# Weight splits issued by a thread of their own, a third buffer for token copies, and later emission times in a planned kernel

## The chip, the cores and the metric

The kernel runs on one core of a Trainium2 chip. The metric is the device time of one launch in microseconds. A core has five engines with a queue each: TensorE (PE, its weight loads PEld), VectorE (DVE), ScalarE (ACT), GpSimd (POOL) and SyncE (SP), which here issues nearly all DMAs. An engine works through its queue in the order in which the program emitted the instructions; where one waits, those behind it wait too.

## What is computed

One inference step of a hybrid encoder layer on 512 prompt frames and 32 sample frames (544 columns), with model width 1024:

```
u    = RMSNorm(h)
proj = u @ w_in                      # 102 column blocks of 128
SSD:  conv -> silu -> state-space recurrence (16 heads x 64, state 128) -> gated RMSNorm with silu(z)
GLA:  4 heads, per-channel forget gate, recurrence -> head RMSNorm times silu(gate)
RWKV: 16 heads x 64, delta rule S_t = S diag(w) - (S kk)(kk a)^T + v k^T -> LayerNorm, bonus, silu(gate)
m    = sum_i sigmoid(merge_i) * (o_i @ P_i)
h    = h + m @ w_out
h    = h + CrossAttention(RMSNorm(h), memory)      # 256 memory tokens
y    = RMSNorm_final(h)
```

The memory's keys and values are computed first. All states are outputs too.

## The kernel before

**The planner.** `body` emits the whole program from cooperating Python generators, called threads here. `Sched` keeps a modelled time for each engine and for the DMAs, and every emitted instruction moves its engine's time on. `Sched.run` resumes the first thread in order of priority (lowest number first) whose wait is over by the modelled time of PE. A thread gives up its turn by `yield`: with a number it sleeps for so many modelled nanoseconds, with a function it sleeps until that is true. `S.at(a)` is the modelled time until tile `a` is written, for a DMA its modelled landing. None of this exists on the chip: the threads decide only in which order instructions stand in the engines' queues. What an instruction truly waits for are semaphores on its operands and on its output buffer's earlier readers.

**Dense blocks.** The 166 weight blocks of 1024x128 (512 KB each) pass through `dense`, the thread of lowest priority (9). Float32 products are made of three float32r products: a high part `wh` and a low part `wl = w - wh` of the weights, and the same two parts of the activations. A block over 544 columns is two halves of 24 matmuls. `load_w` issues the DMA into one of three `wraw` buffers, `split_w` makes the parts: ACT copies `wraw` to `wh`, and a small thread `low` of priority -1 then has DVE subtract. `commit` keeps a list `ahead` of loaded blocks; it takes from three queues in order (jobs of the stage, convolution blocks, and `fill`: 56 gate blocks that depend on `u` alone, of which the last 8 are held back for the end of the second stage). `take` removes from `ahead` the first block whose input is ready and splits it. In `dense`, `more(1)` takes the next block at two places: at the top of the loop, after a block is finished, and right after a block is begun. After each 5 matmuls (`GRAIN`) the thread gives up its turn, and so other threads' small matmuls come in between.

**Stages.** 0 to 65 us: memory keys and values, RMSNorm. 65 to about 660: RWKV in eight pairs of heads, by five threads. `rw_A` prepares a pair (key norms, decays, scan, products of a pair's tokens), and its helper `tokens` transposes three operands on PE (`ptk`), copies them by ACT into a buffer `tm`, and stores them by four DMAs each into the slot tile `NK`; a last copy `t8` (named `t` in the profile) takes the tail tokens through the same ring of buffers, `TMB = 2` of them. Only then does `rw_A` begin the next pair (`w2h`, then `sq`, `k` and the norm matmuls `pn`). `rw_I` inverts triangular 32x32 blocks on POOL (31 steps of `im` and `td`), `rw_J` loads the inverse as `TT`, has DVE transpose it (`x`, L1122) and finishes the 64x64 inverse on PE, `rw_C` runs the recurrence over 9 chunks, `rw_N` normalises. From about 660 to 925: GLA and SSD, beside the convolution blocks, the query and key blocks of GLA and what is left of `fill`. From 925: `gates` (priority 1) loads each branch's result `yt` and gate `gt` (272 KB each, `gt` in 3 buffers, two tiles ahead), multiplies them on DVE and splits the product into parts `o__`; first RWKV (`gated`), then GLA (`gated`), then SSD (`ssd_norm`, which also sums squares, and splits only after the last RWKV projection). The output projections `prwkv`, `pgla`, `pssd` need all eight tiles of their branch; each half block is gated by DVE with a loaded `mgt` into `macc`. Then `wout`, `wq`, attention and `wo` follow, whose weights are kept in parts `wr`.

`S.at` and the ring of a tile tag are what the change turns on:

```
def at(self, *aps):
    return max(0.0, max(self.since(a, 0) for a in aps) - self.t["pe"])
...
if c % W["GRAIN"] == 0 and c < 24:
    commit()
    yield None
```

Of the kernel before, what the change touches and what calls it, by code (L numbers as in the profile page):

```python
# [11 lines left out]
AF = mybir.ActivationFunctionType  # L12
# [34 lines left out]
       ("a", "v"): 145.0, ("a", "p"): 170.0, ("v", "a"): 130.0, ("v", "p"): 155.0, ("p", "v"): 70.0, ("p", "a"): 65.0,  # L47
       ("a", "q"): 150.0, ("v", "q"): 150.0, ("p", "q"): 150.0, ("v", "v"): 127.0, ("a", "a"): 153.0, ("p", "p"): 102.0}

W = dict(HOLD1=0, HOLD2=8, CALM=3000, EARLY1=1, DEPTH1=3, EARLY2=2, FAIR=1500, GRAIN=5, IS=900.0, IE=0, NQ=3000, XL=2, SG=6, PRW=800.0, R2=0.0, DE=2500.0, T2=0, FA=900.0, XM=3000.0, WARM=12, KM=1500.0)  # L50


class Cols:
# [286 lines left out]
def body(tc, I, O):  # L340
    nc = tc.nc
    S = Sched(nc)
# [17 lines left out]
    with tc.manual_schedule(), \  # L360
# [107 lines left out]
        ahead = []  # L468
# [20 lines left out]
        def split_w(j):  # L489
            blk = j["blk"]  # L490
            if blk in spl or blk in splitting:
                return
            tag, w = raw.pop(blk)
            if "res" in j:
                h, l = (pools["res"][1].tile([128, 1088], F32R, name="wr", tag=t) for t in j["res"])
            else:
                k = wn[0] % 2
                wn[0] += 1
                h, l = (base.tile([128, 1088], F32R, name=n_, tag=f"{n_}{k}") for n_ in ("wh", "wl"))
            h, l = h[:, :1024], l[:, :1024]  # L500
            S.act(h, w, AF.Copy)
            hl = tuple(a.rearrange("p (a b) -> p a b", b=128) for a in (h, l))

            def low():
                yield S.at(h)
                S.tt(l, w, f32(h), SUB)
                free_raw[tag] = S.since(w, 1)
                done.add(f"split {blk}")
                spl[blk] = hl

            splitting.add(blk)
            S.add(low(), -1)

        def commit():
            while len(ahead) < look["depth"]:
                q = next((q for q in queues if q and ready(q[0])), None)
                if q is None:
                    if sum(not ready(j) for j in ahead) >= look["early"]:
                        return
                    q = next((q for q in queues if q), None)  # L520
                if q is None or not load_w(q[0]["blk"]):
                    return
                ahead.append(q.pop(0))
# [20 lines left out]
        def dense():  # L544

            nxt = []

            def more(n):
                j = take() if len(nxt) < n else None
                if j is not None:  # L550
                    nxt.append(j)

            while True:
                commit()
                more(1)
                if not nxt:
                    presplit()
                    if not ahead and "end" in done:
                        return
                    yield lambda: any(ready(j) for j in ahead) or (commit() or any(ready(j) for j in ahead)) or "end" in done  # L560
                    continue
                cur = nxt.pop(0)
                commit()
                more(1)
                presplit()
                yield lambda: cur["blk"] in spl
                h, l = spl[cur["blk"]]
                if "res" not in cur:
                    del spl[cur["blk"]]
                    splitting.discard(cur["blk"])  # L570
                x = cur["x"]
                m = cur.get("m", 128)
                hv = cur.get("hv", ((0,) + HV[0], (1,) + HV[1]))
                if "late" in cur:
                    yield lambda: n_late[0] < 3
                    n_late[0] += 1
                for hi, o, w in hv:
                    ps = pd.tile([128, 512], F32, name="pd", tag="pd")
                    yield max(S.at(h), S.since(ps, 1) - S.t["pe"])
                    c = 0  # L580
                    for kb, part in [(kb, part) for kb in range(8) for part in (0, 1)] + [(kb, 2) for kb in range(8)]:
                        if c == 16:
                            yield S.at(l)
                        a = l if part == 2 else h
                        S.mm(ps[:m, :w], a[:, kb, :m], x(kb, o, w)[part % 2], start=c == 0, stop=c == 23)
                        c += 1
                        if c % W["GRAIN"] == 0 and c < 24:
                            commit()
                            yield None
                    if hi == hv[-1][0] and W["T2"]:  # L590
                        commit()
                        more(2)
                    if "late" in cur:
                        S.add(late(cur, ps), -0.5)
                        continue
                    if "ucond" in cur:
                        yield cur["ucond"]
                    cur["use"](hi, ps)
                    done.add(f"{cur['blk']}:{hi}")
                    yield None  # L600
                done.add(cur["blk"])
# [288 lines left out]
            return a.rearrange("p (c t) -> p c t", t=64)  # L890

        HP = ((0, 288), (288, 288))
        TMB = 2

        def rw_A(p):

# [214 lines left out]
        def rw_J(p):  # L1111

            yield has(f"rwJ{p}")
            rwr = pools["rwR"][1]
            d = slot[p % NSLOT]
            nk, tt_ = d["NK"], d["TT"]
            for h in range(2):
                S.dma(out=tt_[h * 64:h * 64 + 64, :, h * 64:h * 64 + 64], in_=rows64(d_scr, h))
            yield S.at(tt_)
            x1 = rwr.tile([128, 8, 32], F32, name="x1", tag="xw")  # L1120
            for h in (0, 64):
                nc.vector.transpose(x1[h:h + 64], tt_[h:h + 64, 0:8, h:h + 32])  # L1122
                S.note("v", 340, (x1[h:h + 64],), (tt_[h:h + 64],))
            yield S.at(x1) + W["XM"]
            ps = yield from bank("pW")
            for c in range(8):
                for h in (0, 64):
                    S.mm(ps[h:h + 64, c * 32:c * 32 + 32], nk[h:h + 32, c, h // 64, h // 32, :], x1[h:h + 32, c, :], True, True)
            w = rwr.tile([128, 8, 32], F32, name="W", tag="xw")
            S.act(w.rearrange("p c j -> p (c j)"), ps[:, :256], AF.Copy)  # L1130
            yield S.at(w)
            ps = yield from bank("pT")
            for c in range(8):
                for h in (0, 64):
                    S.mm(ps[h:h + 32, c * 32:c * 32 + 32], w[h + 32:h + 64, c, :], tt_[h + 32:h + 64, c, h + 32:h + 64], True, True)
            for h in (0, 64):
                S.act(tt_[h:h + 32, 0:8, h + 32:h + 64], ps[h:h + 32, :256].rearrange("p (c t) -> p c t", t=32), AF.Copy)
            done.add(f"rwI{p}")
            yield None
# [536 lines left out]
        def gated(br, t):  # L1676

            yield has(*[f"{dict(rwkv='rg', gla='gg')[br]}{j}" for j in range(8)])
            low = None
            for j, (yt, gt) in enumerate(gate_loads(br)):  # L1680
                yield S.at(yt, gt)
                S.stt(yt, yt, 0.5, gt, MUL, MUL)
                if low:
                    low()
                low = split_o(br, t, j, yt)
                yield S.free("v")
            low()
            done.add(f"O{br}")

        def ssd_norm(t):  # L1690

            gp = pools["gate"][1]
            yield has(*[f"z{j}" for j in range(8)])
            ys, rr = [], []
            for j, (yt, gt) in enumerate(gate_loads("ssd")):
                yield S.at(yt, gt)
                S.stt(yt, yt, 0.5, gt, MUL, MUL)
                if j % 4 == 0:
                    sq = gp.tile([128, T], F32, name="nsq", tag="nsq")
                S.act(gt if j % 4 else sq, yt, AF.Square)  # L1700
                if j % 4:
                    S.tt(sq, sq, gt, ADD)
                ys.append(yt)
                yield S.free("v")
                if j % 4 == 3:
                    yield S.at(sq)
                    r = gp.tile([128, T], F32, name="nrr", tag="nrr", bufs=2)
                    rr.append(r)
                    rstd(r, sq, HV, 512)
            yield has("prwkv7")  # L1710
            low = None
            for j, y in enumerate(ys):
                S.stt(y, y, Pm("g_ssd", j), rr[j // 4], MUL, MUL)
                if low:
                    low()
                low = split_o("ssd", t, j, y)
                yield S.free("v")
            low()
# [404 lines left out]
```

## Time and profile before

| | |
|---|---|
| time, median of 3 runs | 1303.99 us (1301.09 to 1306.32) |
| the profiled execution's own time | 1301.87 us |
| its span, first to last instruction | 1300.1 us |
| PE busy, matmuls | 1260.5 us, 97% |
| PE busy, weight loads | 1215.3 us, 93% |
| DVE, ACT, POOL busy | 65%, 48%, 28% |
| mean granted TensorE clock | 0.99 |
| moved by DMA | 181.11 MB, 45.1% of 16 engines' time |

Times in the rows are microseconds from the span's start. A row of a timeline gives start, duration, engine, line, operation, output<-inputs and shapes, and in brackets how long the engine had been idle and what ended that. A row of the waits gives who waited for whom: total us, times, longest us. Line L245 is the one line from which all plain matmuls are emitted, L278 all ACT work, L284 and L293 most DVE work, L327 all DMAs; the tile names tell them apart.

### The profile page before, as it was taken

How to read it: one execution, taken by the hardware profiler on the slowest of the kernel's cores; microseconds unless marked ns; L12 is line 12 of the kernel's file. 1: busy time of each engine (PE TensorE's matmuls, PEld its weight loads, DVE VectorE, ACT ScalarE, POOL GpSimd, SP SyncE). 2: the span in 40 equal slices, each digit the busy share in tenths (PEclk: the TensorE clock that was granted, in tenths of full speed). 3: DMA queues.
4: the chain of work that ended last, by engine and by line, in shares of the span. 5: the costliest groups of instructions: out<-in, count | busy, mean ns of one | idle time of the engine just before them, and what ended most of it. 6: DMA issues, size and time to landing. Idle time of an engine off the chain costs nothing.

```text
span 1300.1 us, 27497 instructions
## 1 busy us (share of the span) xinstructions
PE 1260.5 (97%) x10848; PEld 1215.3 (93%) x10848; DVE 838.8 (65%) x1666; ACT 627.3 (48%) x1191; POOL 361.6 (28%) x706
## 2 busy tenths in 40 slices
PE   8999989999999999999999999989999999999997
PEld 8999989999998999999999999978999999999997
DVE  6857747675858586844456586877665846575543
ACT  6664534557373637444364646364444423544422
POOL 0012837375656645551001062432100000000000
PEclk8999989999999999999999999999999999999999
DMA  8644462727363635364253243343887445540302
GB/s 291 190 129 111 131 147 64 182 75 183 84 167 96 156 96 151 99 174 134 101 191 114 76 127 109 103 135 114 277 311 251 141 144 181 171 146 25 106 17 70
DMA packets 170385, 181.11 MB, mean 139 GB/s; under 512 B 100480, under 2 KB 123104, under 8 KB 170128
## 3 DMA queue, kind: packets, MB, share of 16 engines
q1 hardware_dynamic: 169824, 178.68, 45.1%
q8 instruction: 86, 1.41, 0.5%
q10 hardware_dynamic: 432, 0.67, 0.2%
q14 instruction: 43, 0.35, 0.1%
HBM read 136.27 MB, written 35.39 MB: 132 GB/s over the span
## 4 chain that ended last, share of the span: by engine, by line
PE 54%; DVE 7%; ACT 2%; issue 1%; POOL 1%; DMA 0%; POOLq 0%; DVEq 0%; ACTq 0%; SPq 0%
PE pd L245 42%; PE pc L245 2%; PE psc L245 1%; PE pov L245 1%; PE py L245 1%; PE pO L245 1%; DVE wl L284 1%; DVE acc L293 1%; PE ph L245 1%; DVE AR L284 1%; PE pT L242 1%; PE pss L245 1%; PE pS L245 0%; DVE seg L299 0%; PE pp L245 0%
## 5 line engine op out<-in xcount | busy, mean ns | idle before, releaser
L245 PE MATMUL pd<-ul,wh 128*128 128x272 f32 (+1 forms) x1632 | 434.5, 295 | 0.0
L245 PE MATMUL pd<-uh,wh 128*128 128x272 f32 (+1 forms) x1632 | 431.1, 294 | 3.1 <-ACT wh L278 2.3
L245 PEld LDWEIGHTS pd<-uh,wh 128*128 128x128 f32 (+1 forms) x1632 | 307.1, 188 | 6.9 <-ACT wh L278 2.8
L245 PEld LDWEIGHTS pd<-ul,wh 128*128 128x128 f32 (+1 forms) x1632 | 307.4, 188 | 3.0 <-issue 1.5
L245 PE MATMUL pd<-uh,wl 128*128 128x272 f32 (+1 forms) x1632 | 251.4, 291 | 0.0
L245 PEld LDWEIGHTS pd<-uh,wl 128*128 128x128 f32 (+1 forms) x1632 | 219.9, 188 | 2.7 <-issue 1.4
L284 DVE TENSOR_TENSOR wl<-wraw,wh 128x1024 fp32r<-128x1024 f32 (+1 forms) x143 | 182.2, 1277 | 29.7 <-ACT wh L278 28.2
L278 ACT ACTIVATE wh<-wraw 128x1024 fp32r<-128x1024 f32 (+1 forms) x143 | 149.3, 1047 | 44.9 <-PE pd L245 27.4
L284 POOL TENSOR_TENSOR im<-td,nd 108x84 f32<-108x84 f32 (+23 forms) x248 | 110.8, 447 | 176.4 <-DMA td<-in_eye 86.5
L245 PE MATMUL pd<-uh,wr 128*128 128x256 f32 (+1 forms) x768 | 148.6, 291 | 1.4 <-ACT uh L278 1.4
L245 PEld LDWEIGHTS pd<-uh,wr 128*128 128x128 f32 x768 | 121.0, 188 | 3.0 <-ACT uh L278 1.6
L284 POOL TENSOR_TENSOR td<-td,im 108x84 f32<-108x84 f32 (+23 forms) x248 | 117.5, 474 | 19.4
L284 POOL TENSOR_TENSOR macc<-macc,hrs 128x288 f32<-128x288 f32 x3 | 2.3, 792 | 372.6 <-DVE macc L293 372.6
L245 PE MATMUL pd<-ul,wr 128*128 128x256 f32 (+1 forms) x384 | 100.2, 292 | 0.1
L245 PEld LDWEIGHTS pd<-ul,wr 128*128 128x128 f32 x384 | 72.4, 188 | 1.0 <-issue 0.4
L278 ACT ACTIVATE lerpA<-pd,par 128x272 f32<-128x272 f32 x50 | 24.4, 487 | 71.1 <-PE pd L245 60.2
L278 ACT ACTIVATE fg<-pd 128x272 f32<-128x272 f32 x64 | 25.3, 397 | 66.2 <-PE pd L245 56.0
L293 DVE SCALAR_TENSOR_TENSOR Sb<-Sb,GC,pc 64x64 f32<-64x64 f32 x128 | 35.7, 279 | 32.3 <-PE pc L245 30.3
L278 ACT ACTIVATE NK<-pc 128x128 f32<-128x128 f32 x136 | 30.5, 275 | 46.3 <-DVE Sb L293 44.5
L278 ACT ACT_TABLE_LOAD x39 | 50.0, 1283 | 3.9 <-DVE tB L284 1.6
L293 DVE SCALAR_TENSOR_TENSOR fg<-fg,pd 128x272 f32<-128x272 f32 x48 | 20.7, 433 | 47.5 <-ACT fg L278 47.2
L278 ACT ACTIVATE fg<-pd,dpar 128x272 f32<-128x272 f32 x48 | 23.3, 486 | 51.0 <-PE pd L245 46.6
(469 smaller groups left out, 2461.1 us busy)
## 6 DMA issues: line engine op xcount, KB each, us to landing
wraw<-in_wall SPq DMA_DIRECT2D x165, 512.0 KB
g_mg<-fg SPq DMA_DIRECT2D x24, 272.0 KB
mgt<-g_mg SPq DMA_DIRECT2D x24, 272.0 KB
NK<-tm SPq DMA_DIRECT2D x96, 64.0 KB
ab<-acs_d SPq DMA_DIRECT2D x8, 512.0 KB
nd<-n_scr SPq DMA_DIRECT2D x24, 144.0 KB
n_scr<-NK SPq DMA_DIRECT2D x16, 144.0 KB
TT<-d_scr SPq DMA_DIRECT2D x16, 144.0 KB
```

Of the source, the lines that this page charges most:

```text
L242: self.nc.tensor.transpose(out, lhsT, rhs)
L245: self.nc.tensor.matmul(out, lhsT, rhs, start=start, stop=stop, skip_group_check=shared)
L278: self.nc.scalar.activation(out=out, in_=in_, func=f, scale=scale, bias=bias)
L284: eng.tensor_tensor(out=out, in0=a, in1=b, op=op)
L293: self.nc.vector.scalar_tensor_tensor(out=out, in0=a, scalar=s, in1=b, op0=op0, op1=op1)
```

## The change

Five edits. The thread `low` now waits until the raw weights have landed by the plan and only then emits ACT's copy to the high part; before, `split_w` emitted the copy at once. Inside a block, after each 5 matmuls, `dense` takes the next block if it has none, if the first block in `ahead` is ready, and if that block's load has landed by the plan. The ring for token copies has 3 buffers instead of 2. The thread `rw_J` sleeps 1500 ns more after the planned landing of `TT`. The gating of GLA and of SSD sleeps 2000 ns more for each of its 16 tiles after the planned landing of `yt` and `gt`.

```
-W = dict(..., KM=1500.0)
+W = dict(..., KM=1500.0, TM=1500.0, GM=2000.0)
...
 def split_w(j):
...
-            S.act(h, w, AF.Copy)
             hl = tuple(a.rearrange("p (a b) -> p a b", b=128) for a in (h, l))
 
             def low():
+                yield S.at(w)
+                S.act(h, w, AF.Copy)
                 yield S.at(h)
                 S.tt(l, w, f32(h), SUB)
...
                         if c % W["GRAIN"] == 0 and c < 24:
                             commit()
+                            if not nxt and any(ready(j) and (j["blk"] in spl or j["blk"] in splitting or S.at(raw[j["blk"]][1]) == 0.0) for j in ahead[:1]):
+                                more(1)
                             yield None
...
-        TMB = 2
+        TMB = 3
...
-            yield S.at(tt_)
+            yield S.at(tt_) + W["TM"]
             x1 = rwr.tile([128, 8, 32], F32, name="x1", tag="xw")
...
-                yield S.at(yt, gt)
+                yield S.at(yt, gt) + (W["GM"] if br == "gla" else 0.0)
...
-                yield S.at(yt, gt)
+                yield S.at(yt, gt) + W["GM"]
```

## Rows read from the trace of the kernel before

**Rows 1.** The page: busy time of each engine, and the granted clock in 40 slices of the span (tenths of full speed).

```profile
PE 1260.5 (97%) x10848; PEld 1215.3 (93%) x10848; DVE 838.8 (65%) x1666; ACT 627.3 (48%) x1191; POOL 361.6 (28%) x706
PEclk8999989999999999999999999999999999999999
```

**Rows 2.** Windows by stage: length, busy us (and count) of PE, PEld, DVE, ACT and POOL, granted clock, DMA share, GB/s.

```profile
65.00:100.00 35.00, 35.00 (x282) 35.00 (x281) 20.73 (x39) 21.89 (x37) 6.58 (x11) 1.00 0.40 120
100.00:660.00 560.00, 543.54 (x5155) 524.67 (x5155) 363.09 (x753) 277.32 (x562) 273.80 (x572) 0.99 0.47 127
660.00:925.00 265.00, 258.74 (x2180) 241.97 (x2179) 186.81 (x367) 141.20 (x251) 77.22 (x102) 0.99 0.39 125
925.00:960.00 35.00, 32.81 (x255) 32.62 (x254) 22.62 (x29) 17.12 (x28) 0.00 (x0) 0.97 0.99 348
```

**Rows 3.** Waits of PE over the whole span, the first four of the list.

```profile
PE pc L245 <- DVE R L284: 4.4, 7, 1.2
PE pn L245 <- ACT k L278: 4.1, 1, 4.1
PE pd L245 <- DVE kv L284: 2.5, 1, 2.5
...
PE pd L245 <- ACT wh L278: 2.3, 3, 1.5
```

**Rows 4.** Timelines around 184 us: ACT's copies of the second pair, the DMAs of its token copies on SP, and PE.

```profile
167.37 1.09 ACT L278 ACTIVATE tm<-ptk 128x512 f32<-128x512 f32 x2 [1.85 <-PE ptk L242]
...
181.55 5.28 SPq L327 DMA_DIRECT2D NK<-tm  x8
...
185.83 0.48 ACT L278 ACTIVATE t<-ptk 64x384 f32<-64x384 f32 x1 [5.64 <-DMA NK<-tm]
...
187.32 0.68 ACT L278 ACTIVATE k<-sq 128x576 fp32r<-128x576 f32 x1
...
188.05 0.61 PE L245 MATMUL pn<-k,blk 128*128 128x288 f32 x1 [4.10 <-ACT k L278]
```

**Rows 5.** Two windows of PE alone in which the granted clock is at its lower level: length, busy us (count), clock, DMA share, GB/s.

```profile
186.40:193.10 6.70, 4.86 (x20) 0.50 0.87 219
...
957.80:961.10 3.30, 3.30 (x17) 0.50 0.99 333
```

**Rows 6.** ACT's timeline: the last token copy `tm` and the tail copy `t` of a further pair.

```profile
366.21 0.60 ACT L278 ACTIVATE tm<-ptk 128x512 f32<-128x512 f32 x1 [0.29 <-PE ptk L242]
...
376.75 0.47 ACT L278 ACTIVATE t<-ptk 64x384 f32<-64x384 f32 x1
```

**Rows 7.** Two places where PE ran out of dense work: DVE's rows that made the next block ready, ACT's copies of its weights, PE's first matmul.

```profile
906.13 1.12 DVE L293 SCALAR_TENSOR_TENSOR ys<-xs,par,py 128x128 f32<-128x128 f32 x4 [0.16 <-PE py L245]
...
914.77 0.40 PE L245 MATMUL pd<-uh,wh 128*128 128x272 f32 x1 [1.52 <-ACT wh L278]
...
949.85 0.72 DVE L284 TENSOR_TENSOR o__12118<-yt,o__12118 128x544 fp32r<-128x544 f32 x1
...
955.12 2.00 ACT L278 ACTIVATE wh<-wraw 128x1024 fp32r<-128x1024 f32 x2
...
956.27 0.49 PE L245 MATMUL pd<-o__11911,wh 128*128 128x272 f32 x2 [2.19 <-issue]
```

**Rows 8.** What follows there: SP's issue of the first merge gates, and DVE's first use of them.

```profile
958.98 0.90 SPq L327 DMA_DIRECT2D mgt<-g_mg  x2
...
965.09 0.78 DVE L293 SCALAR_TENSOR_TENSOR macc<-mgt,pd 128x272 f32<-128x272 f32 x2 [5.26 <-DMA mgt<-g_mg]
```

**Rows 9.** The gating of GLA and SSD: its 16 products (duration in ns, first and last start), DVE's last low part of SSD, and PE's first matmul of the SSD projection.

```profile
L293 DVE SCALAR_TENSOR_TENSOR yt<-yt,gt x16: 716/719/726, 951.8 to 1009.1; 128x544 f32<-128x544 f32 x16
...
1034.39 0.72 DVE L284 TENSOR_TENSOR o__13071<-yt,o__13071 128x544 fp32r<-128x544 f32 x1
...
1055.91 0.41 PE L245 MATMUL pd<-o__12857,wh 128*128 128x272 f32 x2
```

**Rows 10.** Timelines of ACT and DVE near 20 us.

```profile
19.14 1.06 ACT L278 ACTIVATE wh<-wraw 128x1024 fp32r<-128x1024 f32 x1 [2.98 <-DMA wraw<-in_wall]
...
21.04 1.09 DVE L284 TENSOR_TENSOR kv<-pd,rsm 128x256 f32<-128x256 f32 x3 [2.42 <-ACT rsm L278]
```

**Rows 11.** Waits of ACT and DVE for the loads that the change is about.

```profile
ACT wh L278 <- DMA wraw<-in_wall: 10.6, 5, 3.0
...
DVE x L1122 <- DMA TT<-d_scr: 7.8, 7, 2.2
...
ACT wr L278 <- DMA wraw<-in_wall: 6.3, 6, 2.3
...
DVE yt L293 <- DMA gt<-g_gla: 2.1, 2, 1.3
```

**Rows 12.** PE's timeline in the second stage, where it had no dense block.

```profile
846.85 0.63 PE L242 MATMUL pT<-con,g_gl 128*128 128x128 f32 x4 [1.30 <-DVE g_gl L284]
...
859.16 0.49 PE L245 MATMUL pO<-g_qe,gS 128*128 128x128 f32 x2 [1.23 <-DVE gS L305]
```

**Rows 13.** Two of the 25 us windows of the RWKV stage, that with the fullest DVE and that with the most PE idle time but for the one of rows 4 (columns as in rows 2), and POOL's steps of the inverse (ns: least, median, most).

```profile
200.00:225.00 25.00, 24.77 (x195) 24.01 (x195) 22.96 (x47) 9.48 (x21) 20.88 (x33) 1.00 0.23 77
...
400.00:425.00 25.00, 23.14 (x196) 21.83 (x197) 19.78 (x48) 6.91 (x17) 10.23 (x21) 1.00 0.42 115
...
L284 POOL TENSOR_TENSOR td<-td,im x248: 222/348/2068, 126.3 to 590.5; 108x84 f32<-108x84 f32 x12, 108x54 f32<-108x54 f32 x8, 108x90 f32<-108x90 f32 x8, 108x72 f32<-108x72 f32 x8
```

More of the change, by code (lines that the diff above doesn't have):

```diff
@@ L48 @@
        ("a", "q"): 150.0, ("v", "q"): 150.0, ("p", "q"): 150.0, ("v", "v"): 127.0, ("a", "a"): 153.0, ("p", "p"): 102.0}
-W = dict(HOLD1=0, HOLD2=8, CALM=3000, EARLY1=1, DEPTH1=3, EARLY2=2, FAIR=1500, GRAIN=5, IS=900.0, IE=0, NQ=3000, XL=2, SG=6, PRW=800.0, R2=0.0, DE=2500.0, T2=0, FA=900.0, XM=3000.0, WARM=12, KM=1500.0)
+W = dict(HOLD1=0, HOLD2=8, CALM=3000, EARLY1=1, DEPTH1=3, EARLY2=2, FAIR=1500, GRAIN=5, IS=900.0, IE=0, NQ=3000, XL=2, SG=6, PRW=800.0, R2=0.0, DE=2500.0, T2=0, FA=900.0, XM=3000.0, WARM=12, KM=1500.0, TM=1500.0, GM=2000.0)
 class Cols:
@@ L500, in split_w @@
             h, l = h[:, :1024], l[:, :1024]
-            S.act(h, w, AF.Copy)
             hl = tuple(a.rearrange("p (a b) -> p a b", b=128) for a in (h, l))
             def low():
+                yield S.at(w)
+                S.act(h, w, AF.Copy)
                 yield S.at(h)
@@ L588, in dense @@
                             commit()
+                            if not nxt and any(ready(j) and (j["blk"] in spl or j["blk"] in splitting or S.at(raw[j["blk"]][1]) == 0.0) for j in ahead[:1]):
+                                more(1)
                             yield None
@@ L892, in body @@
         HP = ((0, 288), (288, 288))
-        TMB = 2
+        TMB = 3
         def rw_A(p):
@@ L1118, in rw_J @@
                 S.dma(out=tt_[h * 64:h * 64 + 64, :, h * 64:h * 64 + 64], in_=rows64(d_scr, h))
-            yield S.at(tt_)
+            yield S.at(tt_) + W["TM"]
             x1 = rwr.tile([128, 8, 32], F32, name="x1", tag="xw")
@@ L1680, in gated @@
             for j, (yt, gt) in enumerate(gate_loads(br)):
-                yield S.at(yt, gt)
+                yield S.at(yt, gt) + (W["GM"] if br == "gla" else 0.0)
                 S.stt(yt, yt, 0.5, gt, MUL, MUL)
@@ L1695, in ssd_norm @@
             for j, (yt, gt) in enumerate(gate_loads("ssd")):
-                yield S.at(yt, gt)
+                yield S.at(yt, gt) + W["GM"]
                 S.stt(yt, yt, 0.5, gt, MUL, MUL)
```

## The prediction, made blind

> **What bounds the kernel now.** I read the page first, then PE's waits, then windows by stage, then the timelines around each of PE's stops. On the page PE is busy for 97% of the span and no other engine for more than 65%, and the clock line is at 9 but for the first and the sixth slice [rows 1]. So the kernel is bound by PE's work, and what can be won is PE's idle time: 1300.1 - 1260.5 = 39.6 us, and what the lower clock costs after some of the stops. The windows say where: 16.5 us idle in the RWKV stage, 6.3 in the GLA and SSD stage, 2.2 in the 35 us of the gating [rows 2]; the rest is at the start and at the very end. The list of PE's waits [rows 3] shows that few are long: a norm matmul waits 4.1 us for ACT's `k`, a dense block 2.5 us for DVE's `kv`, and dense blocks 2.3 us for `wh`. No engine is overloaded at these places; each is an instruction that stood in the wrong place of a queue.
>
> **Third buffer for token copies.** The stop at 184 us reads backwards like this [rows 4]. PE's `pn` waits for ACT's `k`. ACT reached `k` late because the tail copy `t` before it in ACT's queue stood for 5.64 us, until the DMAs `NK<-tm` were done. With two buffers `t` overwrites the one from which the copy before the last is being stored, and SP issued those eight stores only from 181.55 on. With three, `t` takes the buffer of the pair's first copy, whose own copy stands two before. So the wait of 5.64 us goes, `k` moves ahead by more than the 4.10 us that PE idled, and the 4.10 us go whole. What is late next is DVE's second part of `k`, 0.2 us; I count nothing for it. Just after the stop the granted clock stood at 0.50, that is 1.2 instead of 2.4 GHz, and PE worked 4.86 us there [rows 5]; at the upper level that work takes half, so 2.4 us come back. Sum: -6.5 us.
>
> The same ring also holds up the thread `rw_A`: in this pair `t` ends 18 us after the last `tm` began, and in another it starts 10.5 us after it without a wait that the profile shows [rows 4, 6]; there the plan itself waits for the stores, and the next pair begins only after `t`. All pairs will begin earlier. As PE is full of dense work in this stage this gives no time by itself: it uses fewer fill blocks early and leaves them for the second stage. I take the stage as some 30 us shorter (a slot is free only when the recurrence of three pairs before is done, so not all of 8 x 10 us), which is five blocks.
>
> What those blocks are worth: in the second stage PE idled 1.30 and 1.23 us at places where it had no dense block [rows 12]. Between 0 and -2.5 us; I take half, -1.2. What they cost: the same DVE work in 530 instead of 560 us. The stage now idles 16.5 us, 12.4 of it outside the stop [rows 2, 4]. I take +1.5, bounds 0 and, as a rival below, the worst window.
>
> **Taking the next block inside a block.** Twice PE ran out because the next block's input became ready while the current block was running, and its weights were split only after that block [rows 7]. The products that free the held fill blocks were ready at 907 us, but PE started the block at 914.77 after 1.52 us idle. RWKV's last gated part was ready at 950.6; ACT split the first projection's weights at 955.12, and PE idled 2.19 us. With the new test the split comes at the next group of 5 matmuls, and both stops go: 1.52 + 2.19 = 3.7 us, and half of the 3.30 us at the lower clock after the second [rows 5], 1.65. Sum: -5.4 us. The split moves ACT's and DVE's work (about 1 and 1.2 us) ahead of the current block's evacuation, and the next 512 KB load with it. Where PE is always busy a matmul takes 35.00 / 282 = 0.124 us [rows 2], a half block of 24 thus 3.0 us, and three PSUM buffers hide a delay of 1 us. What is late next is the merge gate: issued at 958.98, landed by 965.09 [rows 8]. PE may run three halves, 9 us, before DVE must have used it, until about 963 if PE starts at 954.1. If the issue moves ahead by the same 2.2 us it is in time; if it stays, up to 2.2 us of the gain are given back. I take it as in time, since it is issued when the first half is evacuated.
>
> **High part by the thread.** ACT waits 10.6 us in 5 places and 6.3 us in 6 places for raw weights [rows 11] and holds back what stands behind. Only one of these shows in PE: at 19.14 ACT stood 2.98 us, the norm factor `rsm` behind it was late, DVE's `kv` after it, and PE waited 2.5 us for the bank [rows 3, 10]. But the block that PE wanted then needed those same weights, whose split ended at 20.20; so not the whole wait can go. Bounds 0 and 2.5 us; I take -0.5. On the other side a split emitted after the planned landing can fall behind another ACT operation, and the raw buffer's next load, queued on SP behind the subtraction, comes later too. Behind one `k` of 0.68 us each [rows 4] the 11 places would cost 7.5 us if each were just in time; between taking a block and using it lies a block of 48 matmuls, 6 us, so I take 0.
>
> **Later transposes and later gating.** DVE stood 7.8 us in 7 places for `TT` and 2.1 us in 2 for GLA's gates [rows 11], with other work behind it; PE idled at none of these. TM adds 1.5 us to each of 8 inverses; PE has fill blocks to do meanwhile, so 0; without that cover 12 us at most. GM adds 2 us to each of 16 tiles in one thread. Their products run from 951.8 to 1009.1, that is 3.8 us each; SSD's parts are done at 1035.1, and PE needs them at 1055.91, so 20.8 us are free [rows 9], 17.0 after PE loses 3.8 us just before. Bounds: nothing, if the waits only replace waits for the landing, and 16 x 2 = 32 us, if they add in full. `gt` has three buffers, so three loads are under way, and 2 us added to a chain over three tiles make 0.67 each, 10.7 in all. That is hidden; I take 0.
>
> **The sum.** -6.5 - 1.2 + 1.5 - 5.4 - 0.5 = -12.1 us. Against the profiled execution's own 1301.9 us this gives 1289.8; its time was 2.1 us under the median of the three runs, so I predict 1292 us.
>
> **The rivals.** First, *the gating of SSD comes too late*. If GM adds in full, the parts are ready 32 - 17.0 = 15.0 us after PE wants them, at a point with no other dense work: 1292 + 15 = 1307. It decides from 17.0 / 16 = 1.1 us added per tile. For it speaks that one thread handles all tiles in turn; against it the pace of 3.8 us, longer than the 2 us added. Chance 0.12.
>
> Second, *the first stage gets too dense*, which ends slower. DVE is busy 363 of 560 us there, and PE's most frequent wait is for DVE's `R` [rows 2, 3]. If every 25 us idle like the worst ordinary window, 1.86 us [rows 13], that is 22.4 x 1.86 = 41.7 us instead of 12.4, +29.3: 1292 - 1.5 + 29.3 = 1320. It makes the kernel slower by over 0.5% when the mean reaches 1.45 us (12.4 + 1.5 + 18.5 = 32.4 us over 22.4 windows). Against it: the window with the fullest DVE, 22.96 of 25 us, idles 0.23 [rows 13]. POOL's steps speak for it: `td` takes 222 ns at least and 2068 at most [rows 13], so something holds POOL at times. The Trainium skill (SBUF — State Buffer, "SBUF: two separate sides") says that a DVE instruction with two SBUF inputs and a GpSimd instruction that reads SBUF take a shared port pair as an exclusive lock, so that one of them blocks; the spread agrees with it, and by that rule closer packing would lengthen the inverse, and the recurrence that waits for it, as in this rival. Chance 0.13.
>
> Third, *the stop only moves*: with the orders all shifted, another norm or projection meets an equal wait, or the second place of rows 7 isn't reached in time. Then only one group of the gains is left, 5.4 or 6.5 us: 1304 - 6 = 1298, within 0.5%. Chance 0.16.
>
> How much room there is, is itself in doubt: by PE's matmuls 39.6 us are idle, by its weight loads 1300.1 - 1215.3 = 84.8. The Trainium skill (Perfetto Trace Analysis, its opening note) says that matmul busy time is the bad measure and the weight loads' share the good one; by that rule more than my sum could be won.
>
> **How the numbers follow.** The forecast has 0.59, the rivals 0.12, 0.13 and 0.16. A difference under 0.5%, 6.5 us, can hardly be told from none here. The forecast alone lies between 1283 (all bounds in its favour: 2.0 more at the start, 1.3 in the second stage, 1.5 for no crowding, and 4, a sixth of the 26.8 us for which ACT and DVE stand in rows 11, should some of these count for PE after all) and 1297. With the first and third rival the range is 1283 to 1307; above it lies most of the second rival, below it little. Faster by over 0.5%: the forecast, and a little of the third rival, 0.60; within 0.5%: most of the third and the first, 0.25; slower: the second, and a late gating with further loss, 0.15.
>
> **What would show it.** Right: `t` no longer waits for `NK<-tm`, and the last `t` comes well before 571 us; the 4.1 us wait of `pn` and the lower clock after it are gone; PE starts the first projection without a gap of 2 us; ACT's waits for `wraw` and DVE's for `TT` shrink; PE's idle time falls from 39.6 to about 29 us. Wrong: a gap of PE before the SSD projection; more idle time from 100 to 640 us in waits for `R` or `Sb`; a new stop of several us with the lower clock behind it; PE's `pd` waiting for `wh` more often than 3 times.

## The result and the profile after

The changed kernel took 1293.3 us (median; 1292.3 to 1293.5) and the kernel before 1304.6 beside it (1301.1 to 1306.3): a ratio of 0.9928, 95% interval 0.9905 to 0.9951 (the two medians alone give 0.991, inside it). Predicted were 1292 us. The profiled execution took 1293.31 us with a span of 1291.5, against 1301.87 and 1300.1 before.

The page after, PE's busy time and the granted clock in 40 slices [rows 1]:

```profile
PE 1256.5 (97%) x10848; PEld 1214.8 (94%) x10848; DVE 837.9 (65%) x1666; ACT 623.5 (48%) x1189; POOL 363.4 (28%) x706
PEclk9999989999999999999999999999999999999999
```

PE's idle time is 1291.5 - 1256.5 = 35.0 us, where it was 39.6. The prediction had about 29. The windows by stage, with PE alone (length, busy us and count, clock, DMA share, GB/s), say where it fell [rows 2]:

```profile
100.00:660.00 560.00, 541.42 (x5152) 0.99 0.47 130
660.00:925.00 265.00, 262.36 (x2198) 0.99 0.40 123
925.00:960.00 35.00, 35.00 (x282) 1.00 0.92 326
```

The first window idles 18.6 us, where it was 16.5: nothing was won in the RWKV stage, in which I had placed half of the gain. The second went from 6.3 to 2.6 and the third from 2.2 to 0. The other 4.0 us are busy time; what made the same 10848 matmuls shorter I did not find.

PE's longest waits after [rows 3]:

```profile
PE pT L245 <- ACT W L278: 4.3, 1, 4.3
PE pd L245 <- ACT wh L278: 4.1, 4, 1.3
PE pc L245 <- DVE R L284: 3.9, 4, 1.7
PE pc L245 <- DVE Sb L293: 3.7, 1, 3.7
```

Here `W` belongs to the inverse, and `R` and `Sb` to the recurrence. `pn <- k` and `pd <- kv` are off the head of the list, as predicted, but a stop of the same size stands 7 us earlier. This is its neighbourhood in the timelines of SP, ACT and PE (start, duration, then the idle time before the instruction and what ended it):

```profile
162.56 1.31 SPq L327 DMA_DIRECT2D d_scr<-td  x3
...
166.99 2.85 SPq L327 DMA_DIRECT2D nd<-n_scr  x3
...
171.25 2.62 SPq L327 DMA_DIRECT2D NK<-tm  x4
173.97 0.55 SPq L327 DMA_DIRECT2D wraw<-in_wall  x1
...
177.67 1.06 ACT L278 ACTIVATE wh<-wraw 128x1024 fp32r<-128x1024 f32 x1 [7.25 <-DMA wraw<-in_wall]
...
180.30 0.37 ACT L278 ACTIVATE W<-pW 128x256 f32<-128x256 f32 x1
...
180.72 1.06 PE L245 MATMUL pT<-TT,W 32*32 32x32 f32 x32 [4.25 <-ACT W L278]
```

Read backwards: PE's `pT` waits for ACT's `W`; ACT is late because the split `wh` before it stood 7.25 us for its raw weights; and SP issued that load only at 173.97, after a run of DMAs that begins at 162.56 with the stores of the inverse's result `td`. In the kernel before, the token copy `t` stood there for its buffer [rows 4]; now a weight split stands there for its load. The clock fell to its lower level again, too, as it did before [rows 5]:

```profile
178.70:185.50 6.80, 4.78 (x68) 0.50 0.60 169
```

ACT's waits for raw weights at `wh` rose from 10.6 us in 5 places [rows 11] to this:

```profile
ACT wh L278 <- DMA wraw<-in_wall: 31.5, 12, 7.2
```

Those at `wr` are off the list; with one at `hs`, of 2.2 us, the sum is 33.7 us, where it was 16.9.

Two more rows matter below (count, duration in ns, first and last start). The first, by the tile `t`, is ACT's copy in all eight pairs; the last began at 571.6 before:

```profile
L278 ACT ACTIVATE t<-ptk x8: 472/481/486, 115.2 to 537.8; 64x384 f32<-64x384 f32 x8
```

The second, by the tile `g_ssd`, gives SP's stores of the eight `z` blocks, the last fill blocks that may run early; the last started at 823.8 before, and it was the only one after 705 us:

```profile
L327 SPq DMA_DIRECT2D g_ssd<-fg x8: 319/323/382, 657.0 to 862.4; - x8
```

### The profile page after: what moved, and what is told of

The parts are those of the page before. It is cut to its first block, busy times and chain, and to the rows that moved or that the text cites. A ratio compares the mean times of both kernels' runs of the same rounds, so it can differ in the third digit from the quotient of the medians.

```text
span 1291.5 us, 27500 instructions
## 1 busy us (share of the span) xinstructions
PE 1256.5 (97%) x10848; PEld 1214.8 (94%) x10848; DVE 837.9 (65%) x1666; ACT 623.5 (48%) x1189; POOL 363.4 (28%) x706
## 4 chain that ended last, share of the span: by engine, by line
PE 60%; DVE 4%; ACT 1%; issue 1%; POOL 0%; POOLq 0%; ACTq 0%; DVEq 0%
PE pd L245 46%; PE pc L245 3%; PE psc L245 1%; PE pO L245 1%; PE py L245 1%; PE pov L245 1%; PE ph L245 1%; DVE wl L284 1%; PE pS L245 1%; PE pss L245 1%; PE pT L242 1%; DVE acc L293 0%; PE pl L245 0%; PE pp L245 0%; DVE AR L284 0%
## 5 line engine op out<-in xcount | busy, mean ns | idle before, releaser
L284 DVE TENSOR_TENSOR wl<-wraw,wh 128x1024 fp32r<-128x1024 f32 (+1 forms) x143 | 176.8, 1238 | 43.4 <-ACT wh L278 42.8
L284 POOL TENSOR_TENSOR td<-td,im 108x84 f32<-108x84 f32 (+23 forms) x248 | 114.3, 461 | 19.4
L278 ACT ACTIVATE NK<-pc 128x128 f32<-128x128 f32 x136 | 30.4, 274 | 30.8 <-DVE Sb L293 27.3
```

The costliest lines, as they stand in the source:

```text
L278: self.nc.scalar.activation(out=out, in_=in_, func=f, scale=scale, bias=bias)
L284: eng.tensor_tensor(out=out, in0=a, in1=b, op=op)
```

## Each part alone, on the kernel before

```diff
 a1_ring3     TMB = 2 -> 3
 a2_midtake   + if not nxt and any(ready(j) and ... for j in ahead[:1]): more(1)
 a3_thread    S.act(h, w, AF.Copy) moved into low(), behind yield S.at(w)
 a4_times     TM = 1500, GM = 2000
```

**The third buffer alone.** Expected:

> The kernel before with the third buffer for token copies alone. By the sum: the tail copy never waits for the stores, the stop of 4.1 us near 184 us and the lower clock behind it (2.4 us) are gone, and the second stage idles a little less: 6 us faster, about 1298.5 us, PE idle 33 to 35 us. By the rival that the stop only moves, as the trace of the changed kernel suggests (SP's queue is late with the stores, and the next weight load stands behind them): another stop of 3 to 6 us with the lower clock behind it between 150 and 400 us, in which ACT stands for raw weights; the gain is then 0 to 3 us, 1302 to 1305 us.

Measured: 1314.5 us, ratio 1.0102 [1.0073, 1.0131]. It is slower by 13 us. The largest stop is at the same place again, behind a third ACT instruction:

```profile
190.22 0.40 ACT L278 ACTIVATE fg<-pd 128x272 f32<-128x272 f32 x1 [13.14 <-DMA g_rwkv<-fg]
...
191.15 0.60 PE L245 MATMUL pd<-uh,wh 128*128 128x272 f32 x1 [7.38 <-DVE fg L293]
```

Here, in ACT's and PE's timelines, a gate copy `fg` waits 13.14 us for the store of the tile that it overwrites. That store, too, is one of SP's. Neither expectation has this time. A second stop, of 5.47 us at 419, stands where DVE waits 3.71 us for `TT`, the wait that TM is meant for.

**The mid-block take alone.** Expected:

> The kernel before with the taking of the next block inside a block alone. By the sum: PE's gaps of 1.52 us (before the first held fill block) and 2.19 us (before the first RWKV projection) go, and with the second the lower clock behind it, 1.65 us: 5.4 us faster, 1299 us; the first 800 us of the trace as before. By the rival that the merge gate is late next: the second gap comes back as a wait of PE for a PSUM bank some 9 us later, 3 us faster only, 1301.5 us.

Measured: 1293.6 us, ratio 0.9958 [0.9936, 0.9980], which is 5.5 us. The gaps at 913 and 954 us are gone [rows 7], and no wait for the merge gate came in their place: PE idles 0.4 us from 925 to 960.

**The thread alone.** Expected:

> The kernel before with the high part emitted by the thread alone. By the sum: PE's wait for kv at 19 us shrinks from 2.5 to about 0.5 us, nothing else: 1304 us, between 1302 and 1305. ACT's waits for raw weights, 16.9 us in all, should shrink if the planned landing is right. By the rival that the plan's landings are too early when SP is behind: ACT's waits for raw weights do not shrink, or grow as in the changed kernel, where ACT stood 31.5 us for wh; the time is then within 3 us of the kernel before, either way.

Measured: 1298.7 us, ratio 0.9991 [0.9967, 1.0014]. PE's stop at 19 us fell from 2.55 to 0.47 us; ACT's waits for raw weights hardly shrank (16.9 to 16.0 us in all), and the time is that of the kernel before within the interval, as the rival has it.

**The added times alone.** Expected:

> The kernel before with the two later times alone (1500 ns at the inverse's transpose, 2000 ns at the gating of GLA and SSD). By the sum: 0, 1303 to 1306 us; DVE's wait of 7.8 us for TT goes, the SSD parts are ready about 11 us later against PE's first SSD projection, so that 9 to 10 of the 20.8 us are left. By the rival of the late gating: 32 us later, PE stands some 11 us before the SSD projection, 1316 us.

Measured: 1315.9 us, ratio 1.0115 [1.0083, 1.0146]: slower by 15 us. The RWKV stage ended 10 us later, all `z` blocks were used by 698 us, and PE stopped 7.4 us near 916 us where no dense block was left. The time is the rival's 1316, but not its cause: before the SSD projection, where the late gating would show, PE has no gap over 0.3 us.

By the ratios the four add up to 13 - 5.5 - 1 + 15 = +21 us (the -1 is not clear of noise), and together they give -9. So the parts act on one another, and the next runs take one away at a time.

## One part taken away from the changed kernel

**The ring back to two buffers (TMB = 2).** Expected:

> The changed kernel with two buffers for token copies again (TMB = 2), all else as changed. Theory A, the parts add: alone the third buffer cost 13 us, so without it the kernel takes 1293 - 13 = 1280 us. Theory B, the ring pays only beside TM (alone it brought DVE stops at TT and a stage that was only 4 us shorter, while with TM the stage was 16 us shorter and blocks were left for the second stage): without it the RWKV stage ends later than in the changed kernel (its last gate product after 652 us instead of 636), no block is left after 800 us, PE idles over 6 us from 660 to 925, and the time is 1300 us or more. Prediction's own term: 6.5 us at the stop, so 1299 to 1300.

Measured: 1315.5 us, ratio 1.0115 [1.0088, 1.0143]. Theory A, that the parts add, falls by 35 us; theory B holds in all its signs. The last step of the recurrence ended at 666 us, where it was 637 with the ring. The stores of the `z` blocks:

```profile
L327 SPq DMA_DIRECT2D g_ssd<-fg x8: 319/320/381, 653.1 to 701.8; - x8
```

PE's window of the second stage:

```profile
660.00:925.00 265.00, 252.69 (x2088) 0.98 0.37 119
```

PE's largest stop, from its timeline:

```profile
926.16 1.98 PE L245 MATMUL py<-seg,xc 128*64 128x128 f32 x16 [6.32 <-DVE seg L284]
```

The ring's use beside the other parts is to be seen here. Without it the stage is 29 us longer, PE fills these 29 us with `z` blocks, and none is left after 702; in the second stage PE then idles 12.3 us, where the changed kernel with its four blocks after 830 idles 2.6. Over the whole span PE idles 8.3 us more than in the changed kernel and is busy for 12.6 us more; of the latter the lower clock makes some 8, estimated as half of the difference between 34.1 and 17.9 us of work at the lower level. The wait for `seg` (DVE itself waits there for the load of `ab`) has no like in the changed kernel, where PE's idle time of this stage is 2.6 us in all.

**Without the mid-block take.** Expected:

> The changed kernel without the taking of the next block inside a block. Theory A, the part's worth is local (the gaps before the second stage's dense blocks and before the first projection): the gaps near 910 and 950 us are back, 1.5 and 2.2 us with lower clock after the second, and the time is 1293 + 5.4 = 1299 us, as in the run of this part alone, which gave 5.5. Theory B, with z blocks left over in the second stage the first of these gaps has cover: only the gating's gap comes back, 1293 + 3.8 = 1297. If the time is that of the changed kernel within 1 us, the part owed its gain to the new order that it made.

Measured: 1296.7 us, ratio 0.9966 [0.9951, 0.9982], 0.0038 x 1301 = 4.9 us over the changed kernel's ratio; the two intervals just touch. One gap came back, not two, and larger:

```profile
910.65 0.59 PE L245 MATMUL pd<-uh,wh 128*128 128x272 f32 x1 [4.20 <-ACT wh L278]
```

The size fits both theories. The place is A's first gap; its second, before the first projection, did not come back, and B had it the other way round.

**Without the thread.** Expected:

> The changed kernel with the high part emitted as before, at once, and not by the thread. Theory A: the thread's copy is worth the kv stop at 19 us alone, 2.1 us, so 1295 us, with ACT's waits for raw weights as long as in the changed kernel (some 30 us in 12 places), since these come from loads that stand behind token stores on SP. Theory B: the thread holds other orders up; without it the waits for raw weights fall to 15 us or less and the time to 1290.

Measured: 1299.5 us, ratio 0.9990 [0.9968, 1.0011]; its ten times spread from 1292.6 to 1305.4, and the profiled one is the lowest. So the size is uncertain, some 8 us by the ratios. The waits for raw weights fell to 17.2 us in 10 places, nearly as B has it, but the time rose, as A has it, and more than A has it. The stop at 19 us is back with 2.78 us. The stop near 180 us is there again, three times as long and again behind `fg`:

```profile
188.55 0.40 ACT L278 ACTIVATE fg<-pd 128x272 f32<-128x272 f32 x1 [16.13 <-DMA g_rwkv<-fg]
...
190.85 1.07 PE L245 MATMUL pT<-TT,W 32*32 32x32 f32 x32 [11.98 <-ACT W L278]
```

**Without GM.** Expected:

> The changed kernel with GM = 0, no added time at the gates of GLA and SSD. Theory A (GM is hidden but for the last microsecond): the two halves of the gating end some 10 to 17 us earlier, about 1010 instead of 1026, the 0.9 us gap of PE at 1048 goes, and the time is 1292. Theory B (GM keeps gate products away from ACT and DVE work that PE needs in the second stage): DVE's waits for gates return and PE idles more from 660 to 960, so 1297 or more.

Measured: 1290.8 us, ratio 0.9914 [0.9893, 0.9936]. This is theory A, though by the intervals it can't be told from the changed kernel. The last high part of SSD's gating starts at 1020.26 without GM. With it, in the changed kernel, the same part and PE's first matmul of the SSD projection are:

```profile
1047.54 0.66 ACT L278 ACTIVATE o__13297<-yt 128x544 fp32r<-128x544 f32 x1 [1.50 <-DVE yt L293]
...
1049.20 0.52 PE L245 MATMUL pd<-o__13099,wh 128*128 128x272 f32 x2 [0.89 <-ACT wh L278]
```

GM thus moves the end of the gating by 1047.54 - 1020.26 = 27.3 us, more than theory A's 10 to 17, and uses up all the room before PE needs the parts: 0.89 us are missing.

**Without TM.** Expected:

> The changed kernel with TM = 0, no added time at the inverse's transpose. Theory A (the ring needs TM: with three buffers and no TM, DVE stood 11.7 us in 7 places for the inverse's result, and PE stopped 5.5 us once behind it): DVE's waits for TT come back, to 8 us or more in all, PE stops over 3 us at one of them with lower clock after it, and the time is 1300 us or more. Theory B (TM is hidden, as in the prediction's sum): the time is that of the changed kernel, 1291 to 1295.

Measured: 1289.5 us, ratio 0.9914 [0.9889, 0.9938]; theory B for the time. DVE's waits for the inverse's result did come back, as A has it, and PE's waits for `R` grew with them from 3.9 us:

```profile
DVE x L1125 <- DMA TT<-d_scr: 13.6, 8, 4.1
```

The first of PE's list:

```profile
PE pc L245 <- DVE R L284: 9.4, 8, 2.9
```

PE's stops of over 3 us, which A had too, did not come: the longest is 2.95. The recurrence ended at 628 instead of 637 us and six `z` blocks were left instead of four, so that PE idled 0.04 us from 660 to 925. The one pays for the other.

## One root for the stops near 180 us

In ten of the eleven kernels so far PE stops for 2.9 to 12.0 us between 179 and 192 us, with ACT ahead of it waiting for a DMA that SP issued late: `t` before, in a2_midtake and in a3_thread, `wh` after the change, in m2_nomid and in m6_noGM, `fg` in a1_ring3, a4_times, m1_ring2 and m3_nothread. Ahead of these issues SP had stood for POOL's `td`, as in the kernel before:

```profile
166.60 1.30 SPq L327 DMA_DIRECT2D d_scr<-td  x3
...
177.59 2.17 SPq L327 DMA_DIRECT2D nd<-n_scr  x3
```

It issued the stores of `td` at 166.60 after 4.7 us of standing; it stood 4.5 us more, up to 177.59, for the copy `n_scr`, issued behind them, and the token stores that held up `t` were the eighth group of issues from the stores of `td` on [rows 4]. The eleventh kernel, m5_noTM, shows what a late load needs to become a stop. There SP issues the weight load even later than after the change, but ACT had done `W` at 171.83, before it stood for the load, and PE's longest stop near 180 us is 2.09:

```profile
175.37 0.55 SPq L327 DMA_DIRECT2D wraw<-in_wall  x1
...
179.21 1.06 ACT L278 ACTIVATE wh<-wraw 128x1024 fp32r<-128x1024 f32 x1 [2.89 <-DMA wraw<-in_wall]
```

SP's waits for `td` from 100 to 660 us in all (us, times, longest), before:

```profile
SPq L327 <- POOL td L284: 49.8, 8, 12.5
```

and after:

```profile
SPq L327 <- POOL td L284: 25.4, 6, 8.2
```

The Trainium skill (DMA: Bandwidth & Descriptors, "Anatomy of one DMA — SWDGE (gpsimd) path") says that the DMA engines don't wait on semaphores, so that any such wait is made by the issuing sequencer before it sends the DMA off. It says so of another issuing path; here SP's rows agree, since after the change the load of 173.97 stands behind the stores of `td`, which waited 7.7 us; its own buffer had been free since 157.5, when DVE had read it for `wl`. Between the two SP waited 1.6 us more, for these stores to land, and 1.1 us for DVE.

**The stores of `td` later in the plan.** The base is the changed kernel without GM.

```diff
-S.store(out=blocks(d_scr)[:, g:32:3], in_=td[...])
+S.stores.append((blocks(d_scr)[:, g:32:3], td[...], max(S.since(td, 0, "q"), S.since(d_scr, 1, "q")) + 6000.0))
+S.stores.sort(key=lambda x: x[2])
```

> The changed kernel with GM = 0 (which took 1290.8), and with the stores of the inverse's result td given a place in SP's queue 6 us later in the plan; nothing else in the plan's costs is touched. Theory A (weight loads come late because SP stands for POOL's td, 26 us in 6 places, up to 7.9 us, with token stores and weight loads behind it): SP's waits for td fall below 8 us, ACT's waits for raw weights after 100 us fall from about 23 us to below 10, PE's stop of 4.3 us at 177 and that of 2.6 us at 365 go together with the lower clock after them, and the time is 1290.8 - 4.3 - 2.6 - 3.4 (half of two stretches of 3.4 us at the lower clock) = 1280 to 1284. Theory B (every new order meets some wait of this size): other stops of 3 to 7 us stand elsewhere and the time is 1288 to 1294. Theory C (the recurrence waits for the later result): the RWKV stage ends over 10 us later, no dense block is left after 800 us, and the time is over 1300.

Measured: 1278.3 us, ratio 0.9836 [0.9805, 0.9867], beside 0.9914 of its base: 0.0078 x 1300 = 10 us by the ratios. This is theory A but for one sign, 2 us below its range. The profiled execution, the slowest of its four, took 1283.9 with a span of 1282.1. SP's wait for `td` from 100 to 660 us:

```profile
SPq L327 <- POOL td L284: 0.6, 1, 0.6
```

PE's window of the RWKV stage:

```profile
100.00:660.00 560.00, 548.20 (x5225) 0.99 0.46 132
```

PE's longest waits:

```profile
PE pd L245 <- ACT wh L278: 5.2, 4, 2.0
PE pc L245 <- DVE R L284: 3.7, 5, 1.4
```

The stage idles 11.8 us instead of 18.1 in the base, no stop is longer than 2.04, and ACT's waits for raw weights from 100 to 660 us fell from 22.9 to 9.6 us. Against theory C, the stores' delay costs the recurrence nothing: those of the second pair start at 168.00 instead of 163.19 in the base, and still the last step ends at 622 instead of 638 us. The sign that failed is the clock, which still fell once near 180 us, behind an idle time of 1.38 us at 182:

```profile
184.90:191.70 6.80, 6.80 (x90) 0.50 0.46 157
```

This version beats both kernels.

**A margin at the split instead.** On the same base, ACT is kept from standing for late weights without mending why they are late.

```diff
-yield S.at(w)
+y = S.at(w)
+yield y + 3000.0 if y > 0 and "ux" in done else y
```

> The changed kernel with GM = 0, and with the thread waiting 3 us more than the plan's landing time before it emits a weight's high part, after the first layer norm is done. Theory A (what costs is that ACT stands for late weights with PE's other work behind it): ACT's waits for raw weights after 100 us fall from about 23 us to below 8, the stop of 4.3 us at 177 shrinks below 2, and the time is 1283 to 1286. Theory B (the dense block then comes late instead, since its weights are split 3 us later): PE waits for wh and wl in more than 7 places and the time is 1292 or more.

Measured: 1306.8 us, ratio 1.0039 [1.0023, 1.0056]: theory B in its result (PE waits for `wh` and `wl` in 8 places). ACT's waits for raw weights after 100 us fell to 6.5 us, but at the old place `fg` waited 15.61 us for its store, and PE stopped for the low part behind it:

```profile
191.37 1.27 PE L245 MATMUL pd<-uh,wl 128*128 128x272 f32 x4 [11.22 <-DVE wl L284]
```

**The later stores alone, on the kernel before.** The same edit, with two buffers and nothing else.

> The kernel before, with one thing of the last experiment alone: the stores of the inverse's result td have a place in SP's queue 6 us later in the plan. Theory A (one root: in the kernel before, too, SP stands from 161.9 to 166.6 for POOL's td and then issues its followers, and the token stores that t waits for come only at 181.55): SP's waits for td fall from 49.8 us to below 10, t no longer waits 5.6 us, the stop of 4.1 us at 184 and the lower clock after it go without a third buffer, and the time is 1300 - 6.5 = 1291 to 1296. Theory B (the third buffer is needed, since the ring itself holds the pairs up): t still waits over 3 us somewhere, and the time is 1298 to 1304. Theory C (the later result lengthens the stage, which has no ring to shorten it): the last N step ends after 662 us, the z blocks are all used by 705, PE stops over 5 us near 915 as in the two runs of 1315, and the time is over 1308.

Measured: 1306.0 us, ratio 1.0049 [1.0031, 1.0068]. SP's wait for `td` from 100 to 660 us:

```profile
SPq L327 <- POOL td L284: 5.0, 4, 2.2
```

PE's windows of the two stages:

```profile
100.00:660.00 560.00, 551.21 (x5235) 1.00 0.47 130
660.00:925.00 265.00, 249.74 (x2027) 0.94 0.36 115
```

The stores of the `z` blocks, and PE's largest stop from its timeline:

```profile
L327 SPq DMA_DIRECT2D g_ssd<-fg x8: 319/320/362, 638.8 to 687.4; - x8
```

```profile
915.68 1.97 PE L245 MATMUL py<-seg,xc 128*64 128x128 f32 x16 [7.06 <-DVE seg L284]
```

Theory A holds for the place: the stop at 184 us went without a third buffer, `t` waits 1.6 us at most, and the stage idles 8.8 us instead of 16.5. The time lies between theory B's 1304 and theory C's 1308. C's signs at the end are there, the `z` blocks used up and the stop near 915, but not their cause: the recurrence ends at 652 us, as before (653). In a stage of the same length, PE did 7.7 us more, and since the only work at hand was fill, it used up the `z` blocks by 687. The second stage idles 15.3 us instead of 6.3 [rows 2], 9.0 more, at a clock of 0.94. What was won in the first stage was paid back in the second.

Eight of the profiles side by side, worked out from their timelines (end of the recurrence: DVE's last `cs<-NK`; `z` blocks left after 705 us) and windows (PE idle):

| kernel | recurrence ends | z left | idle 100:660 | idle 660:925 | ratio |
|---|---|---|---|---|---|
| before | 653 | 1 | 16.5 | 6.3 | 1 |
| changed | 637 | 4 | 18.6 | 2.6 | 0.9928 |
| a1_ring3 | 649 | 4 | 26.2 | 4.5 | 1.0102 |
| a4_times | 663 | 0 | 15.9 | 15.0 | 1.0115 |
| m1_ring2 | 666 | 0 | 15.4 | 12.3 | 1.0115 |
| b1_later | 652 | 0 | 8.8 | 15.3 | 1.0049 |
| m5_noTM | 628 | 6 | 21.9 | 0.0 | 0.9914 |
| e1_later | 622 | 4 | 11.8 | 2.6 | 0.9836 |

With no block left the second stage idles 12 to 15 us, with four or more 0 to 5. Of the profiles that are not in the table, m2_nomid idles 6.8 us with four blocks, 4.2 of them in the gap that the mid-block take closes, and e2_margin idles 1.2 us with six, but 23.6 in the first stage. That is the one thing; the stops behind SP are the other. a1_ring3 had the blocks and lost on the stops; b1_later had no stops and lost on the blocks.

## Why the prediction was right, point by point

By the medians the forecast is 1.3 us off. By the profiled executions, against which the sum was made, 8.6 us of span went where the terms gave 12.1: idle time fell by 4.6 us where they gave 8.0, and busy time by 4.0 us where they gave 4.05, but not by the clock that I had put it down to: PE worked 18.6 us at the lower level before and 17.9 after, worth 0.35 us. By the ratio the gain is 9.4 us. So the time is right while the largest term is wrong, and that it came out so near is in part luck: the 6.5 us of the stop were not won, and 4.0 us of busy time whose cause is not known stand in their place. All four signs of being wrong that the prediction named are in the trace: a gap of 0.89 us before the SSD projection, 7.6 us instead of 5.8 in waits for `R` and `Sb`, a new stop of 4.25 us with the lower clock behind it, and four waits of `pd` for `wh`. Of its signs of being right, ACT's waits for `wraw` grew, and PE idles 35 us and not 29.

Halving the work at the lower clock was a little too much: in the changed kernel dense matmuls start every 0.125 us at 174 us and every 0.225 at 183, so 0.44 of the time comes back and not 0.5.

**Third buffer, -6.5 us at the stop.** The mechanism was read rightly up to its last link: `t` no longer waits, and `k` is early. What failed is the sentence that puts DVE's second part of `k` next, 0.2 us later. It looked for the next instruction behind the waiting one and not at the queue that had issued its DMA: SP, having stood for `td`, had a run of issues to make up, and the next of ACT's instructions that depended on one of them took the place of `t`. A stop of 4.25 us stands where 4.10 stood. For this term the third rival happened, "the stop only moves". And b1_later shows a second fault: even where the stop does go, PE's idle time is not simply won, because the stage has a length of its own, and PE only uses up its fill sooner.

**The stage 30 us shorter, worth 1.2 us.** The length was right only beside the other parts: 666 to 637 us is 29. Alone, on the kernel before, the ring made the stage 4 us shorter (653 to 649), and all the parts together 16, or 25 without TM (628). The worth was the term most mis-sized. I priced the blocks by the two small gaps of the kernel before [rows 12], which had just one block left; m1_ring2 has none, and by the ratios takes (1.0115 - 0.9928) x 1301 = 24 us more than the changed kernel. Not all of that is the blocks' price: 9.7 us are idle time of the second stage, and some 5 are the lower clock there (13.4 us of work at the lower level from 847 to 933, where it was 3.4). The blocks are a stock, and these two profiles and those without blocks in the table say that its price rises at the point where it runs out.

**Crowding, +1.5 us.** Right in size: outside its longest stop the stage idles 18.6 - 4.25 = 14.4 us, where it was 12.4. But it is not density, since three stops (3.75, 1.96 and 1.75 us) make up 7.5 of it, and the first of these, at 363 us, again stands behind a late weight load. The second rival did not happen: the medians of POOL's steps hardly moved, `td` from 348 [rows 13] to 343 ns and `im` from 336 to 331; the longest `td` fell from 2068 to 1503 and the longest `im` rose from 1522 to 2005. What the rival rests on is there in both kernels, though. Laid beside DVE's timeline, all 121 steps of over 400 ns before, and all 119 after, overlap a DVE instruction with two tensors as inputs; with the subtraction `wl` beside it a step takes 1173 ns in the middle before, without it 334. So the weight splits lengthen the inverse whose end SP stands for.

**Mid-block take, -5.4 us.** Right in size: 5.5 us alone, 4.9 as the part taken away. Right in place alone, where both gaps went; taken away from the changed kernel, one larger gap came back and not two.

**High part by the thread, -0.5 us.** The stop at 19 us fell from 2.55 to 0.45, close to the far bound that I had argued against. A split that falls behind other work cost nothing that I can see. What the term left out is ACT standing longer for raw weights, 33.7 us instead of 16.9, of which one place made the new stop. With the other parts the thread seems to be worth some 8 us, by a run with a wide spread. The instruction that stands near 180 us differs with the thread (`wh`) and without it (`fg`).

**TM and GM, nothing.** Right for the time: without either, the kernel is some 2 us faster, which is within the intervals. But TM is not free of effect: it moves the recurrence's end from 628 to 637 us. And GM's 10.7 us were 27.3, near the bound of 32 where the additions count in full; why the three `gt` buffers don't overlap them was not tried. The first rival, a late gating of SSD, thus stood at its threshold, with a gap of 0.89 us. And alone, on the kernel before, the two times cost 15 us: the stage became 10 us longer, and its stock of blocks, of which one was left, ran out. That the stock is what made the 15 us is read from the table and not tested by itself.

## What to carry to other kernels

Where a planned queue meets a stop, follow the wait past the instruction that stands to the queue that issued its DMA, and to what that queue stood for: removing one victim of a late issuing queue hands the stop to the next, while moving the one store that blocked the queue was worth 10 us beside the other parts, and cost 6 without them. And where PE fills waits from a stock of independent work, count what is left of the stock at the end of the stage: a stop removed early pays only if the chain beside it becomes shorter as well, or the stock lasts.

## What was not expected of the hardware

The issue of a DMA itself takes time on SP: four token stores occupy its queue for 2.62 us (at 171.25 in the changed kernel). So what piles up behind one wait is worked off slowly: from 162.56, when POOL's `td` was done, to 183 us the queue stood for only 3.4 us in four places, and a weight load that needed nothing but its turn was issued 11 us after the wait for `td` had ended.
